# Gate tiles of the V stage loaded in three pieces, the first ones ahead of the last block's gathers

## The chip, the cores and the metric

The kernel runs on one core of a Trainium2 chip. The metric is the time of one execution in microseconds (us), taken on the device; the median of several runs stands for a kernel. The engines are named as in the profile: PE multiplies matrices, PEld loads its weights, DVE and ACT work on tiles element by element, POOL and SP mostly issue transfers here. Transfers (DMA) run on 16 DMA engines that all the issuing queues share.

## What is computed

The reference is one decoder layer on 512 tokens of width 1024: a mixer (state-space heads and latent attention), and then an expert mixer called PEER, which is the part that matters here. Each token picks 128 experts out of 16384 (8 heads, 16 each). With `u_table` and `v_table` of 16384 rows of 1024 numbers:

```python
        u = jnp.take(u_table, expert_idx, axis=0)
        act = jax.nn.gelu(jnp.einsum('td,thkd->thk', xb, u).astype(jnp.float32), approximate=False)
        v = jnp.take(v_table, expert_idx, axis=0)
        return jnp.einsum('thk,thkd->td', (gate * act).astype(xb.dtype), v)
```

## The kernel before

The mixer takes the first quarter of the span. PEER then works in two ways at once. For the first 384 tokens it doesn't gather: it computes the activation of every expert for every token with dense matmuls, multiplies by a gate that is zero for experts that were not picked, and multiplies the result with the whole V table. For the last block of 128 tokens it gathers the picked rows of U and V with indirect transfers on POOL (`gather`, L1534 to L1584) and sums on DVE. In fp32 each matrix is split into a high and a low part, so each product takes three matmuls.

The 16384 experts are cut into 128 chunks of 128. A U step (`u_chunk`) takes one 512 KB piece of U and makes the activations of a chunk for the tokens, 128 experts by 352 numbers, with 24 matmuls. A V step (`v_chunk`, L1678) takes one 512 KB piece of V and adds into six PSUM banks with 18 matmuls. The weights come through one stream (`Stream`, L94): SP issues the load of a raw piece `wir` (L105, three buffers), ACT rounds it to the high part `wih` (L123), DVE subtracts for the low part `wil` (L133). SP issues the next load into a raw buffer when DVE has read it.

Before the V steps the gates are built and stored to memory: `gsp`, 12 groups of 32 tokens by 128 by 128 chunks by 32, and the small `gs0` for the first eight chunks of the last two groups. For a V step they are loaded as a tile `gt`, which holds four chunks for all 12 groups of 32 tokens (128 by 12 by 4 by 32, 768 KB), in two buffers. `load_g(q)` loads the tile of the chunks 4q to 4q+3. For the first two tiles POOL loads the part of the last two groups out of `gs0`. For later tiles SP loads from `gsp`. As long as some groups were multiplied already while the gates were built (`open_(c)` counts the groups that are open at chunk c, up to `ND` = 10), only the open groups and the last two are loaded; from chunk 40 on (tile 10) all 12 are, in one transfer of 768 KB.

`v_prep(c)` (L1622) asks for the tile of c and, at every fourth chunk, for the next one, and multiplies activations by gates into `P` on DVE (L1632; for c from 40 on all in one instruction), with a small copy on ACT (L1636). `v_hi` rounds P to `Ph` on ACT (L1655), `v_lo` makes `Pl` on DVE (L1663), and `v_mm` (L1667) multiplies them with the V piece. In a V step c the order written out is: `v_lo` of the chunk before, `v_prep(c + 2)`, the next weight piece with `item()`, `v_hi(c + 2)`, and 18 matmuls.

The stages in time: until about 810 us mixer, routing, gates and the first U steps; four V steps alone; then U and V steps in turn until the U pieces are used up, near 1300 us; then V steps alone. Beside all of them `pump` advances the gathers of the last block, paced by the steps that are left.

Around the start of the V steps the order is: the generator `gather` runs to its first stop (DVE makes `ac`), then to its second (POOL issues the gathers of rows 0 and 1), then `load_g(0)` and `load_g(1)`, then the gather of row 2, then `refill`, which fetches activations that had been put away in memory (L1402).

Of the kernel before, what the change touches and what calls it, by code (L numbers as in the profile page):

```python
# [49 lines left out]
T_Q = 6.3  # L50
ROWS = 5
ENDU = 11
WV = 0.86
GST = (1, 3, 5, 7)
LOWA = (*range(2, 32, 2), 34, 38)
# [12 lines left out]
def tile_block(ctx: ExitStack, tc: tile.TileContext, I, out):  # L68
    nc = tc.nc
# [20 lines left out]
    def chain(*gs):  # L90
        for g in gs:
            yield from g
# [139 lines left out]
    gsp = dram.tile([NT // 32, 128, 128, 32], F32, name="gsp")  # L232
# [74 lines left out]
    for p in range(2):  # L307
# [11 lines left out]
        for j, cs, act in (((0, slice(0, D), 1), (1, slice(0, D), 1)) if p == 0 else  # L319
                           ((0, slice(0, D), 0), (1, slice(0, 512), 1), (1, slice(512, D), 0))):  # L320
            t = XH[:, 2 * p + j, cs]
# [355 lines left out]
    for i in range(13, 18):  # L677
# [3 lines left out]
        q = qraw[i - 13] = wk.tile([128, S], F32, name="qr", bufs=5)  # L681
# [210 lines left out]
    for st in range(39):  # L892
        h, q = divmod(st, 4)
# [141 lines left out]
    def stage1(m):  # L1035
        yield top16(sc.pop(m), 128, TV4[:, :, m], TI4[:, :, m])
        h = m // 2
        if m % 2:
            cand = rt.tile([128, NB, 88], F32, name="cand")
            for c0, a0, na, w in ((0, 0, 1, 16), (16, 1, 3, 8), (40, 4, 12, 4)):  # L1040
                sh = [128, NB, na, w]
                (V if m == 15 else G).tensor_tensor(
                    cand[:, :, c0:c0 + na * w].rearrange("p h (a b) -> p h a b", a=na),
                    TV4[:, :, m - 1, a0:a0 + na, None].to_broadcast(sh),
                    TV4[:, :, m, None, 0:w].to_broadcast(sh), op=OP.add)
            late_c.append((cand, h))
        if late_c and (m % 2 == 0 or m == 15):
            cand, h = late_c.pop()
            yield (0.7 if m == 15 else 0.0) + top16(cand, 88, TS4[:, :, h], PO4[:, :, h])
# [276 lines left out]
    def pump(g, us):  # L1326
        bal[0] = min(bal[0] + us, us)
        while bal[0] > 0:
            c = next(g, None)
            if c is None:  # L1330
                bal[0] = 0.0
                return False
            bal[0] -= c
        return True
# [61 lines left out]
    def refill():  # L1396
        while away:
            t = act_tile()
            if t is None:
                return  # L1400
            c = away.pop(0)
            G.dma_start(t, asp[c - KEEP])  # L1402
            ACT[c] = t
# [82 lines left out]
    fill = iter(())  # L1486
    for m in range(17):
# [6 lines left out]
        if m:  # L1494
            fill = chain(fill, stage1(m - 1))
# [91 lines left out]
    aps.append(pool("act3"))  # L1587
    fill = gather()
    next(fill)
    next(fill)  # L1590
    gt = {}

    open_ = lambda c: sum(d <= c for d in done)
# [1 line left out]
    def load_g(q):  # L1595
        if q < 32 and q not in gt:
            gt[q] = vst.tile([128, NT // 32, 4, 32], F32, name="gt", bufs=2)
            nb = open_(q * 4)
            part = lambda b0, b1: nc.sync.dma_start(gt[q][:, b0:b1], gsp[b0:b1, :, q * 4:q * 4 + 4, :].rearrange("b j i t -> j b i t"))
            if q < 2:  # L1600
                G.dma_start(gt[q][:, ND:].rearrange("j b i t -> j b (i t)"), gs0[:, q])
            elif nb < ND:
                part(ND, NT // 32)
            if nb:
                part(0, nb if q < 2 or nb < ND else NT // 32)

    for q in range(2):
        load_g(q)
    next(fill)
    refill()  # L1610
    if UO:
# [10 lines left out]
    def v_prep(c):  # L1622
        load_g(c // 4)
        if c % 4 == 0:
            load_g(c // 4 + 1)
        a = ACT.pop(c)
        P = vst.tile([128, NT], F32, name="P", bufs=2)
        nb = open_(c)
        for b0, b1 in ((0, ND + 1),) if nb == ND else ((0, nb), (ND, ND + 1)):
            if b1 > b0:  # L1630
                cs = slice(b0 * 32, b1 * 32)
                V.tensor_tensor(P[:, cs].rearrange("p (b t) -> p b t", t=32), a[:, cs].rearrange("p (b t) -> p b t", t=32),  # L1632
                                gt[c // 4][:, b0:b1, c % 4, :], op=OP.mult)
        if nb < ND:
            A.activation(P[:, nb * 32:ND * 32], a[:, nb * 32:ND * 32], AF.Copy)
        A.activation(P[:, NA:], gt[c // 4][:, ND + 1, c % 4, :], AF.Copy)  # L1636
        if c % 4 == 3:
            gt.pop(c // 4)
        prepared[0] += 1
        return P  # L1640
# [37 lines left out]
    def v_chunk(c):  # L1678
        v_lo()
        P = v_prep(c + 2)  # L1680
        if uc == 128:
            v_hi(c + 2, P)
        hl = item()
        if uc < 128:
            v_hi(c + 2, P)
        for b in range(3):
            v_mm(b, c, hl)
# [3 lines left out]
    for c in range(2):  # L1691
        while uc < PRE - 1 + c:
            u_chunk(uc)
            uc += 1
            if uc > un[0] + 2:
                pump(fill, 2.3)
        v_hi(c, v_prep(c))
        v_lo()
    more = True
    units = lambda: (128 - uc) * 2 + WV * (uc - vc)  # L1700
    fin = None
    while vc <= LASTC:
# [14 lines left out]
        else:  # L1717
            if not GS[1]:
                GS[1:] = units() - ENDU, GS[0]
            left = units()  # L1720
            want = 253 - max(0.0, (256 - GS[2]) * (left - ENDU) / GS[1])
            while more and GS[0] < want:
                more = pump(fill, 0.1)
            if more and left < ENDU:
                more = pump(fill, 1.8)
# [9 lines left out]
    for c in range(LASTC + 1, 128):  # L1735
        v_lo()
        if c + 2 < 128:
            v_hi(c + 2, v_prep(c + 2))
        held[c] = item()
# [135 lines left out]
```

## Time and profile before

| | us |
|---|---|
| median of 3 runs | 1581.57 |
| lowest and highest | 1578.41, 1581.69 |
| profiled execution | 1585.28 |
| its span, first to last instruction | 1583.5 |

The profile is of one execution, so durations are compared with its own span. In the page, the first part gives each engine's busy time, share and instructions. A row of the timeline has start, duration, engine, line, operation, what is written and read, the count, and in brackets the idle time of the engine before it with what ended it. In the waits, a row names who waited for whom, the total, the times and the longest. For a transfer the duration in the timeline is that of its issue; when it has landed is seen by who was released.

### The profile page before, as it was taken

What the parts mean: (1) busy time and instruction counts of PE and PEld (TensorE: products, weight loads), DVE (VectorE), ACT (ScalarE), POOL (GpSimd) and SP (SyncE); (2) the same over time, 40 slices, a digit from 0 to 9 for tenths busy, and PEclk for the clock granted to TensorE, in tenths of its full rate; (3) what the DMA queues carried; (4) which work ended last, traced back from release to release, by engine and by line L of the source; (5) the groups of instructions that cost most, each with busy time, mean ns of one, the idle gap of its engine ahead of it and who ended that gap; (6) DMA issues with size and microseconds to landing.
All of it is one profiled execution on the core that took longest, in us unless ns stands there. A gap on an engine that the chain in (4) does not pass through costs nothing.

```text
span 1583.5 us, 24521 instructions
## 1 busy us (share of the span) xinstructions
PE 1550.6 (98%) x8696; PEld 1361.3 (86%) x8696; DVE 1344.2 (85%) x2620; ACT 767.6 (48%) x1536; POOL 619.2 (39%) x455
## 2 busy tenths in 40 slices
PE   9999999999999999999989999999999999999997
PEld 7887888888888999999988999999988878888886
DVE  8988767747799999999957888888888889998997
ACT  5565476741433547776754444444333344443442
POOL 0000032500245434443225655565555556655510
PEclk9999999999999999999999999999999999999999
DMA  6242122474423568999989999999999999999983
GB/s 252 94 160 90 47 76 63 124 238 145 125 86 101 153 211 299 329 328 340 330 314 313 359 344 351 358 364 351 338 339 352 351 350 348 375 363 349 354 284 145
DMA packets 150442, 407.53 MB, mean 257 GB/s; under 512 B 14360, under 2 KB 55528, under 8 KB 150064
## 3 DMA queue, kind: packets, MB, share of 16 engines
q1 hardware_dynamic: 94160, 208.91, 39.2%
q0 software_dynamic: 50288, 177.80, 31.2%
q10 hardware_dynamic: 5872, 19.27, 3.2%
q8 instruction: 68, 1.11, 0.3%
q14 instruction: 54, 0.44, 0.1%
HBM read 374.63 MB, written 29.19 MB: 255 GB/s over the span
## 4 chain that ended last, share of the span: by engine, by line
PE 79%; DVE 7%; DMA 6%; issue 5%; ACT 2%; POOL 2%; DVEq 0%; ACTq 0%; POOLq 0%
PE pu L86 9%; PE va L1672 9%; PE va L1673 9%; PE va L1676 9%; PE pu L88 9%; PE pu L87 9%; PE pa L87 3%; PE pa L88 3%; PE pa L86 3%; PE pw L87 3%; PE pw L88 3%; PE pw L86 3%; DMA row<-v,ix 2%; POOL row L1550 2%; PE pw L1283 1%
## 5 line engine op out<-in xcount | busy, mean ns | idle before, releaser
L123 ACT ACTIVATE wih<-wir 128x1024 fp32r<-128x1024 f32 (+2 forms) x269 | 277.8, 1033 | 226.7 <-DMA wir<-v 94.6
L133 DVE TENSOR_TENSOR wil<-wir,wih 128x1024 fp32r<-128x1024 f32 (+1 forms) x234 | 283.0, 1212 | 76.7 <-ACT wih L123 55.4
L88 PE MATMUL pu<-XT,wil 128*128 128x336 f32 x1008 | 319.0, 316 | 4.5 <-DVE wil L133 4.5
L1673 PE MATMUL va<-wil,Ph 128*128 128x512 f32 x726 | 284.2, 391 | 0.0
L86 PE MATMUL pu<-XT,wih 128*128 128x336 f32 x864 | 276.5, 320 | 3.0 <-ACT wih L123 3.0
L87 PE MATMUL pu<-XT,wih 128*128 128x336 f32 x864 | 272.8, 316 | 0.0
L1550 POOL DMA_INDIRECT row<-v,ix x128 | 207.2, 1619 | 155.4 <-DVE ac L1571 132.3
L1550 POOL DMA_INDIRECT row<-u,ix x128 | 190.0, 1484 | 159.5 <-DVE row L1565 105.1
L88 PEld LDWEIGHTS pu<-XT,wil 128*128 128x128 f32 x1008 | 189.8, 188 | 5.7 <-DVE wil L133 5.6
L1672 PE MATMUL va<-wih,Ph 128*128 128x512 f32 x462 | 181.6, 393 | 4.3 <-ACT Ph L1655 4.3
L1571 DVE SCALAR_TENSOR_TENSOR ac<-row,hd,ac 128x1024 f32<-128x1024 f32 x128 | 164.1, 1282 | 7.9 <-DMA row<-v,ix 6.1
L86 PEld LDWEIGHTS pu<-XT,wih 128*128 128x128 f32 x864 | 162.7, 188 | 6.5 <-ACT wih L123 4.3
L87 PEld LDWEIGHTS pu<-XT,wih 128*128 128x128 f32 x864 | 163.0, 189 | 2.1
L1673 PEld LDWEIGHTS va<-wil,Ph 128*128 128x128 f32 x726 | 137.2, 189 | 27.3 <-DVE wil L133 0.3
L1565 DVE SCALAR_TENSOR_TENSOR row<-row,XT 128x1024 f32<-128x1024 f32 x128 | 150.4, 1221 | 8.1 <-DMA row<-u,ix 8.0
L1676 PE MATMUL va<-wih,Pl 128*128 128x512 f32 x462 | 143.7, 392 | 2.2 <-DVE Pl L1663 2.2
L133 POOL TENSOR_TENSOR wil<-wir,wih 128x1024 fp32r<-128x1024 f32 (+3 forms) x35 | 72.9, 2089 | 154.7 <-PE pw L88 99.4
L123 ACT ACTIVATE wihx<-wir 128x1024 fp32r<-128x1024 f32 x67 | 71.1, 1062 | 121.1 <-DMA wir<-v 96.5
L1146 POOL DMA_INDIRECT urow<-u,uix x48 | 77.2, 1609 | 115.3 <-DVE urow L1152 108.1
L1655 ACT ACTIVATE Ph<-P 128x384 fp32r<-128x384 f32 x121 | 62.9, 520 | 108.3 <-DVE P L1632 74.3
L133 DVE TENSOR_TENSOR wil<-wir,wihx 128x1024 fp32r<-128x1024 f32 x62 | 75.8, 1223 | 40.5 <-issue 19.2
L1672 PEld LDWEIGHTS va<-wih,Ph 128*128 128x128 f32 x462 | 87.3, 189 | 21.9 <-ACT Ph L1655 4.5
(513 smaller groups left out, 3419.0 us busy)
## 6 DMA issues: line engine op xcount, KB each, us to landing
wir<-ut SPq DMA_DIRECT2D x128, 512.0 KB
wir<-v SPq DMA_DIRECT2D x128, 512.0 KB
gt<-gsp SPq DMA_DIRECT2D x22, 768.0 KB
wir<-wo SPq DMA_DIRECT2D x26, 512.0 KB
wir<-wf SPq DMA_DIRECT2D x18, 512.0 KB
wir<-wqr SPq DMA_DIRECT2D x16, 512.0 KB
gsp<-stg ACTq DMA_DIRECT2D x14, 464.0 KB
de<-acd POOLq DMA_DIRECT2D x8, 512.0 KB
```

What stands on the lines that cost most here:

```text
L86: T.matmul(ps, lh, rh, start=start, stop=False)
L87: T.matmul(ps, lh, rl, start=False, stop=False)
L88: T.matmul(ps, ll, rh, start=False, stop=stop)
L123: A.activation(h, r, AF.Copy)
L133: self.lo(n).tensor_tensor(l, r, h, op=OP.subtract)
L1146: G.indirect_dma_start(out=UR[n], out_offset=None, in_=I["u"], in_offset=bass.IndirectOffsetOnAxis(ap=UR["ix"][:, n:n + 1], axis=0))
L1550: G.indirect_dma_start(out=R[s], out_offset=None, in_=I["u"] if s < 128 else I["v"], in_offset=bass.IndirectOffsetOnAxis(ap=ix3[:, s % 128 ...
L1565: V.scalar_tensor_tensor(wide(r), wide(r), 1.0, x3, op0=OP.mult, op1=OP.mult, accum_out=hd[:, s:s + 1])
L1571: V.scalar_tensor_tensor(ac, r, hd[:, s - 128:s - 127], ac, op0=OP.mult, op1=OP.add)
L1672: T.matmul(va[b][e], Ph[b], h[:, cs], start=c == 0, stop=False)
L1673: T.matmul(va[b][e], Ph[b], l[:, cs], start=False, stop=False)
L1676: T.matmul(va[b][e], Pl[b], h[:, cs], start=False, stop=c == 127)
```

## The change

A number `GP` = 4 is the size of a piece in token groups. Loads on SP are not issued in `load_g` any more but put into a list `more_g`. `step_g` takes one entry off it, issues up to four groups, and puts the rest back at the front; if an entry was small and the next one fits with it into four groups, it issues that one too. `v_prep` calls `step_g` once each time, after `load_g`. A whole tile so goes out as three loads of four groups (256 KB each), with the V steps 4q, 4q+1 and 4q+2 for the tile that is first used by the multiply of chunk 4q+4. At the start of the stage, `load_g(0)`, `load_g(1)` and all that they put on the list now come after the first stop of `gather` and ahead of the second.

```diff
+GP = 4
     fill = gather()
     next(fill)
-    next(fill)
     gt = {}
...
-            part = lambda b0, b1: nc.sync.dma_start(gt[q][:, b0:b1], gsp[b0:b1, :, q * 4:q * 4 + 4, :].rearrange("b j i t -> j b i t"))
+            part = lambda b0, b1: more_g.append((q, b0, b1))
             if q < 2:
                 G.dma_start(gt[q][:, ND:].rearrange("j b i t -> j b (i t)"), gs0[:, q])
...
+    more_g = []
+
+    def step_g():
+        if more_g:
+            q, b0, b1 = more_g.pop(0)
+            m = min(b1, b0 + GP)
+            nc.sync.dma_start(gt[q][:, b0:m], gsp[b0:m, :, q * 4:q * 4 + 4, :].rearrange("b j i t -> j b i t"))
+            if m < b1:
+                more_g.insert(0, (q, m, b1))
+            elif more_g and m - b0 + more_g[0][2] - more_g[0][1] <= GP:
+                step_g()
+
     for q in range(2):
         load_g(q)
+    while more_g:
+        step_g()
+    next(fill)
     next(fill)
     refill()
...
         load_g(c // 4)
         if c % 4 == 0:
             load_g(c // 4 + 1)
+        step_g()
```

## The prediction

> **What bounds the kernel now.** I read the page first, for the engine that has least room.
>
> ```profile
> span 1583.5 us, 24521 instructions
> ...
> PE 1550.6 (98%) x8696; PEld 1361.3 (86%) x8696; DVE 1344.2 (85%) x2620; ACT 767.6 (48%) x1536; POOL 619.2 (39%) x455
> ...
> gt<-gsp SPq DMA_DIRECT2D x22, 768.0 KB
> ```
>
> PE is busy for 98% of the span. A change that touches no matmul can win only the time in which PE stands still or runs at a lower clock. So the second view is that of the waits of PE, asked for in stretches; its columns are the total in us, the times and the longest.
>
> ```profile
> PE va L1672 <- ACT Ph L1655: 4.3, 1, 4.3
> ```
>
> ```profile
> PE pu L88 <- DVE wil L133: 4.5, 4, 2.8
> PE pu L86 <- ACT wih L123: 3.0, 3, 1.2
> PE va L1676 <- DVE Pl L1663: 2.2, 2, 2.0
> ```
>
> The first is the answer for 800 to 830 us, the second that for 1160 to 1310 us. Between 900 and 1160 us, and from 1310 to 1530 us, the view has no row. So PE loses 4.3 us at the first V step and 9.7 us (4.5 + 3.0 + 2.2) in one stretch of 150 us. The third view is the busy time by window: span of the window, then PE, PEld, DVE, ACT, POOL, the granted clock, the DMA share and GB/s.
>
> ```profile
> 820.00:840.00 20.00, 15.74 (x68) 13.00 (x67) 8.22 (x15) 9.39 (x22) 9.46 (x12) 0.91 1.01 377
> 1060.00:1080.00 20.00, 20.00 (x108) 17.98 (x107) 17.42 (x30) 8.71 (x19) 11.45 (x8) 1.00 0.98 365
> 1160.00:1180.00 20.00, 16.55 (x78) 14.46 (x78) 14.09 (x15) 8.10 (x15) 8.18 (x7) 0.91 0.83 298
> 1300.00:1320.00 20.00, 17.98 (x72) 14.17 (x71) 18.73 (x22) 7.13 (x13) 13.80 (x7) 0.91 0.97 348
> 1310.00:1530.00 220.00, 220.00 (x972) 182.17 (x971) 202.95 (x239) 89.94 (x164) 123.70 (x71) 1.00 1.00 356
> ```
>
> The clock falls with the long waits: 0.91 over 20 us is (1 - 0.91) x 20 = 1.8 us of clock in each of three windows, one of the first place and two of the second. What there is to win is therefore 4.3 + 1.8 = 6.1 us at the first step and 9.7 + 2 x 1.8 = 13.3 us in the stretch, 19.4 us together.
>
> The Trainium skill (TensorE: Matmul & The Clock Gate, Part 1, and the table under "Why this matters for your kernels") lets the clock fall after an idle time of about 3.4 us and asks for no gap over some 3 us; by that only the first wait would cost clock, and the sum would be 3.6 us smaller. The trace disagrees: the windows with waits of 2.8 and 2.0 us also show 0.91.
>
> **The first loads of the gates.** The chain of work that ended last, from 812 us on (start, us, what), says why PE waits there.
>
> ```profile
> 812.11 2.08 DMA gs<-stg
> ...
> 815.45 10.45 DMA gt<-gs
> 825.91 0.23 ACT P L1636
> 826.20 0.53 ACT Ph L1655
> 826.78 0.51 PE va L1672
> ```
>
> The timeline of POOL, and that of PE, give the order.
>
> ```profile
> 812.21 1.97 POOL L1550 DMA_INDIRECT row<-u,ix  x1 [28.80 <-DVE ac L1543]
> 814.48 0.96 POOL L1550 DMA_INDIRECT row<-u,ix  x1 [0.30 <-DMA gs<-stg]
> 815.45 1.18 POOL L1601 DMA_DIRECT2D gt<-gs  x2
> 816.93 1.17 POOL L1550 DMA_INDIRECT row<-u,ix  x1 [0.30 <-issue]
> 824.27 2.72 POOL L1402 DMA_DIRECT2D act<-asp  x5 [6.17 <-DMA asp<-aout]
> ```
>
> ```profile
> 822.20 0.32 PE L88 MATMUL pu<-XT,wil 128*128 128x336 f32 x1
> 826.78 0.51 PE L1672 MATMUL va<-wih,Ph 128*128 128x512 f32 x1 [4.26 <-ACT Ph L1655]
> ```
>
> Two gathered rows of 512 KB stand ahead of the two small gate loads (256 KB together) in POOL's queue. The change puts the gate loads first. They can't be issued before the store gs<-stg has landed, at 812.11 + 2.08 = 814.19, so they go out about 1.2 us sooner; what counts is that 1 MB is no longer ahead of them. The packets by queue show when POOL's queue (q0) was served at all: between 812 and 819 us it has no row, and from 819 to 822 us it has this one.
>
> ```profile
> q0 software_dynamic: 142, 0.53, 43.4%
> ```
>
> At 0.53 MB in 3 us, 0.26 MB of gates at the head of the queue take 1.5 us: they are through at about 820.5 us, and land at 820.5 to 822 (up to 1.5 us for the tail is an estimate; gs<-stg took 2.08 us from issue to landing in all). From the landing to the matmul it takes 826.78 - 825.90 = 0.9 us, and PE is free at 822.4, so a landing by 821.5 leaves no wait and one at 822 leaves 0.5 us. The bounds are 6.1 us (no wait) and nothing (the load lands at 825.9 as now, held by the stores that fill the other queues). I take 5.5 us.
>
> What is moved with it: the gathers 0 and 1 go out behind the wait for gs<-stg and behind 1.18 us of gate issues, some 3.5 us later than 812.21. Their cover is the idle 6.17 us of POOL ahead of 824.27 and the first use of a row, which DVE makes here:
>
> ```profile
> 841.66 1.22 DVE L1565 SCALAR_TENSOR_TENSOR row<-row,XT 128x1024 f32<-128x1024 f32 x1
> ```
>
> Even if that comes 6 us sooner, the rows have 18 us. Without this cover each us of delay would be a us of DVE. No gate load on SP is moved at this place: the line L1599 starts with tile 2, at 834 us. What is late next is the following weight piece, whose split on DVE stood behind the same wait and so moves with it. Cost taken: nothing.
>
> **The gate tiles in three pieces.** Each whole tile is a load of 768 KB, on the queue that brings the weights. SP's timeline and ACT's show what it does, and a stretch before has the natural comparison: while few blocks were open, a tile came as two small loads.
>
> ```profile
> 1050.30 0.95 SPq L1599 DMA_DIRECT2D gt<-gsp  x2
> 1052.82 0.34 SPq L105 DMA_DIRECT2D wir<-ut  x1
> ...
> 1216.23 0.43 SPq L1599 DMA_DIRECT2D gt<-gsp  x1
> 1218.56 3.91 SPq L105 DMA_DIRECT2D wir<-ut  x1
> ```
>
> ```profile
> 1061.14 1.06 ACT L123 ACTIVATE wih<-wir 128x1024 fp32r<-128x1024 f32 x1 [1.00 <-DMA wir<-ut]
> ...
> 1233.12 1.06 ACT L123 ACTIVATE wih<-wir 128x1024 fp32r<-128x1024 f32 x1 [7.32 <-DMA wir<-ut]
> ```
>
> ```profile
> gt<-gsp SPq DMA_DIRECT2D x1, 192.0 KB
> gt<-gsp SPq DMA_DIRECT2D x1, 128.0 KB
> ```
>
> Behind 320 KB of gates (192 + 128, the issues of 1050 to 1052 us) a weight piece took 1061.14 - 1052.82 = 8.3 us from its issue to ACT, and PE never waited. Behind 768 KB it took 1233.12 - 1218.56 = 14.6 us, of which SP spent 3.91 instead of 0.34 us in the issue itself, and PE waited behind ACT and DVE. A piece of 256 KB is smaller than that harmless case, but it comes in three V steps of four, and the engines have little spare: a share of 0.98 at 1060 us without a wait, 1.00 in the V-only stretch, again without one. The average load does not change, only its lumps. So the two bounds of this part are 13.3 us (every wait goes) and nothing (the queue is as full as before, and the lateness is only spread). By the nearest row, the 8.3 us, nearly all goes; for the fuller queue I keep 2.3 us of waits and take 11.0 us.
>
> What it adds: two more issues for each of 22 tiles, 44 at the 0.43 us of a whole one, 19 us of SP over 450 us. SP mostly waits for DVE anyway:
>
> ```profile
> SPq L105 <- DVE wil L133: 532.5, 169, 10.8
> ```
>
> (800 to 1560 us), so this costs nothing; without that cover a weight piece would be 0.4 us later. Tiles 2 to 9, with their small loads, change only in order, and no wait of PE stands there. The multiply P on DVE now waits for three landings instead of one, and behind it in DVE's order stand the weight splits and the gathers' sums, for which PE and POOL wait. The last piece is the risk, below.
>
> **Sum.** 5.5 + 11.0 = 16.5 us. The profiled execution took 1585.28 us (a span of 1583.5 and 1.8 around it) and would come to 1568.8; it stands 3.7 us above the median of the runs, 1581.57, from which the forecast is counted: 1565 us.
>
> **Rivals.** *The queue stays full.* In the u and V stretch the DMA share is already near 1, PE asks for the same bytes in fewer us once it no longer waits, and weight pieces come late in small steps instead of one large one. Against it stands that at 1160 to 1180 us the share fell to 0.83 just when PE waited: there was room, at another time. Half or less of the 13.3 us would come, 1 to 6.5 us, with the 5.5 us of the first place 6.5 to 12 us in all: 1569.5 to 1575, chance 0.13. At its end stands a case of its own: with the engines full the splitting gives nothing at all, since every byte still has to pass, and only the 5.5 us come, 1576, chance 0.05. The Trainium skill (Perfetto Trace Analysis, DMA Optimizations) names splitting as a help where the DMA engines are generally idle, which they are not here, at 0.97 to 1.01 in four of the five windows; that rule speaks for this last case, and the share of 0.83 against it.
>
> *The first gate load stays late*, because the stores ahead in the other queues and not the gathers hold it. For it speaks that q0 got nothing before 819 us. Then only 11 us come: 1570.5. Chance 0.07.
>
> *The last piece is late: slower.* In the V-only stretch the third piece goes out two V steps before its use. SP's, DVE's and ACT's rows bound it.
>
> ```profile
> 1327.11 3.56 SPq L105 DMA_DIRECT2D wir<-v  x2
> ...
> 1357.36 0.33 SPq L105 DMA_DIRECT2D wir<-v  x1
> ```
>
> ```profile
> 1339.68 0.52 DVE L1632 TENSOR_TENSOR P<-acts,gt 128x352 f32<-128x352 f32 x1
> ```
>
> ```profile
> 1367.90 1.06 ACT L123 ACTIVATE wihx<-wir 128x1024 fp32r<-128x1024 f32 x1 [4.58 <-DMA wir<-v]
> ```
>
> It would be issued with the second of the two pieces at 1327.11, at about 1330.3, for the multiply at 1339.68: a lead of 9.4 us. The slowest weight piece near by took 1367.90 - 1357.36 = 10.5 us, but behind a whole tile. DVE is busy 203 of 220 us there, so a period of four steps (16.3 us) has 1.2 us to spare. Beyond a landing of 9.4 + 1.2 = 10.6 us each further us is lost on each of 14 tiles. To eat the 16.5 us it must be 11.8 us on the average, to be slower by 3.2 us, 12.0. At 12.5 us the loss is 14 x 1.9 = 26.6, net 10 us slower: 1591.7. A piece of a third of the size makes that unlikely. Chance 0.05.
>
> *It doesn't move the bound*: the waits come back elsewhere and the sum is within 0.2%. Chance 0.05.
>
> **How the numbers follow.** The forecast (13 to 20 us won: 1561.5 to 1568.5) has 0.65. The range takes in the full 19.4 us below with a little for the scatter of the runs, 1560.5, and above the first rival and the second, up to 1575; outside are the slower case, no change, the splitting that gives nothing, and edges of the others, some 0.2 together. 0.2%, 3.2 us, is about what a measurement of this kernel can tell from no change. Faster: 0.65 + 0.13 + 0.05 + 0.07 = 0.90; same 0.05; slower 0.05.
>
> **What would show it.** The wait of PE for Ph near 822 us gone or under 1 us, and 1.00 for the clock there; gt<-gs issued ahead of the first row on POOL. In 1160 to 1310 us the three rows of waits under 3 us together, the weight piece behind a gate piece issued in 0.34 us and landing after some 8 us instead of 14.6. DVE must show no wait of P for gt<-gsp in the V-only stretch. It is wrong if PE's waits in that stretch keep more than half of their 9.7 us, or if new waits of P appear.

## The result, and the profile after

| | before | after |
|---|---|---|
| median, us | 1581.57 (5 runs, 1578.41 to 1582.97) | 1564.49 (5 runs, 1563.93 to 1564.82) |
| profiled execution, us | 1585.28 | 1564.62 |
| its span, us | 1583.5 | 1562.9 |

The ratio of the times is 0.9897, with a 95% interval of 0.9882 to 0.9911: 17.1 us less at the medians. The profiled executions differ by 20.7 us, because the one of before, 1585.28 us, was longer than every one of its five runs. The runs of the changed kernel also lie closer together, 0.9 us from lowest to highest against 4.6 us.

The page of the kernel after, its first part:

```profile
span 1562.9 us, 24588 instructions
...
PE 1544.5 (99%) x8696; PEld 1358.9 (87%) x8696; DVE 1344.5 (86%) x2620; ACT 767.6 (49%) x1536; POOL 595.6 (38%) x455
```

PE does the same 8696 matmuls in 1544.5 instead of 1550.6 us of busy time and with less idle time around them. The mean granted clock of the two executions, 0.999 after and 0.995 before, accounts for that difference in busy time: 0.004 x 1550 = 6.2 us. Where the idle time was, the view of PE's waits, from 800 to 1560 us, now has two rows (total, times, longest):

```profile
PE va L1688 <- ACT Ph L1671: 0.6, 1, 0.6
PE va L1689 <- DVE wil L134: 0.3, 1, 0.3
```

The first is the wait at the first V step, 4.3 us before. The three rows of the u and V stretch, 9.7 us together, are gone. (The code has moved down: L1688 was L1672, L1671 was L1655, L134 was L133.) The windows, with span, PE, PEld, DVE, ACT, POOL, clock, DMA share and GB/s:

```profile
820.00:840.00 20.00, 19.37 (x93) 16.27 (x92) 10.07 (x17) 10.96 (x24) 7.78 (x13) 1.00 1.03 400
...
1160.00:1310.00 150.00, 150.00 (x775) 133.16 (x775) 140.28 (x146) 61.68 (x117) 87.51 (x60) 1.00 1.01 375
...
1310.00:1530.00 220.00, 220.00 (x972) 182.08 (x971) 202.21 (x254) 91.85 (x174) 97.69 (x69) 1.00 0.96 338
```

The clock is 1.00 where it was 0.91, and PE is busy for all of the 150 us in which it had stood still for 9.7. The same window of before had this row:

```profile
1160.00:1310.00 150.00, 140.31 (x710) 122.72 (x710) 126.79 (x129) 56.52 (x109) 78.40 (x56) 0.98 0.95 344
```

So 775 instead of 710 matmuls pass in the same 150 us, and the DMA engines move 375 instead of 344 GB/s to feed them: there was room in the engines, only not at the right time. (The two windows don't hold quite the same steps: the last U matmul starts at 1271 us after the change and at 1288 before.)

The chain of work that ended last shows the first V step (start, us, what):

```profile
814.69 7.21 DMA gt<-gs
...
821.92 0.23 ACT P L1652
...
822.20 0.53 ACT Ph L1671
...
822.78 0.50 PE va L1688
```

The gate load now lands 7.21 us after its issue instead of 10.45, at 821.9. POOL's timeline has it ahead of the first gathered row:

```profile
814.69 1.10 POOL L1601 DMA_DIRECT2D gt<-gs  x2 [31.66 <-DMA gs<-stg]
816.09 1.63 POOL L1551 DMA_INDIRECT row<-u,ix  x1 [0.30 <-issue]
```

And SP's timeline shows a weight piece behind a gate piece, issued in 0.33 us where it took up to 3.91:

```profile
1177.08 0.43 SPq L1613 DMA_DIRECT2D gt<-gsp  x1
1179.52 0.33 SPq L106 DMA_DIRECT2D wir<-ut  x1
```

ACT's timeline has its arrival, which no longer holds anybody up for long:

```profile
1187.87 1.06 ACT L124 ACTIVATE wih<-wir 128x1024 fp32r<-128x1024 f32 x1 [1.19 <-DMA wir<-ut]
```

That is 1187.87 - 1179.52 = 8.4 us from issue to ACT, against 14.6 in the case quoted of before.

### The profile page after: what moved, and what is told of

The parts are those of the page before. It is cut to its first block, busy times and chain, and to the rows that moved or that the text cites. A ratio compares the mean times of both kernels' runs of the same rounds, so it can differ in the third digit from the quotient of the medians.

```text
span 1562.9 us, 24588 instructions
## 1 busy us (share of the span) xinstructions
PE 1544.5 (99%) x8696; PEld 1358.9 (87%) x8696; DVE 1344.5 (86%) x2620; ACT 767.6 (49%) x1536; POOL 595.6 (38%) x455
## 4 chain that ended last, share of the span: by engine, by line
PE 89%; DVE 6%; ACT 2%; DMA 1%; issue 1%; DVEq 0%; ACTq 0%; POOLq 0%
PE pu L87 11%; PE pu L89 10%; PE pu L88 10%; PE va L1688 10%; PE va L1689 10%; PE va L1692 10%; PE pa L89 3%; PE pa L88 3%; PE pa L87 3%; PE pw L88 3%; PE pw L89 3%; PE pw L87 3%; PE pw L1284 1%; PE pw L1285 1%; PE pb L536 1%
## 5 line engine op out<-in xcount | busy, mean ns | idle before, releaser
L134 DVE TENSOR_TENSOR wil<-wir,wih 128x1024 fp32r<-128x1024 f32 (+1 forms) x234 | 282.7, 1210 | 74.4 <-ACT wih L124 45.0
L1551 POOL DMA_INDIRECT row<-v,ix x128 | 191.8, 1498 | 159.3 <-DVE ac L1572 131.2
L1551 POOL DMA_INDIRECT row<-u,ix x128 | 185.8, 1452 | 125.6 <-DVE row L1566 99.0
L1688 PE MATMUL va<-wih,Ph 128*128 128x512 f32 x462 | 180.2, 390 | 0.6 <-ACT Ph L1671 0.6
L134 POOL TENSOR_TENSOR wil<-wir,wih 128x1024 fp32r<-128x1024 f32 (+3 forms) x35 | 72.9, 2089 | 154.3 <-PE pw L89 99.3
L1671 ACT ACTIVATE Ph<-P 128x384 fp32r<-128x384 f32 x121 | 62.6, 518 | 130.7 <-DVE P L1648 65.3
L1147 POOL DMA_INDIRECT urow<-u,uix x48 | 73.2, 1524 | 119.5 <-DVE urow L1153 112.5
L134 DVE TENSOR_TENSOR wil<-wir,wihx 128x1024 fp32r<-128x1024 f32 x62 | 75.7, 1222 | 35.1 <-issue 21.6
L1688 PE MATMUL va<-wihx,Ph 128*128 128x512 f32 x264 | 103.0, 390 | 0.0
```

Of the source, the lines that this page charges most:

```text
L134: self.lo(n).tensor_tensor(l, r, h, op=OP.subtract)
L1147: G.indirect_dma_start(out=UR[n], out_offset=None, in_=I["u"], in_offset=bass.IndirectOffsetOnAxis(ap=UR["ix"][:, n:n + 1], axis=0))
L1551: G.indirect_dma_start(out=R[s], out_offset=None, in_=I["u"] if s < 128 else I["v"], in_offset=bass.IndirectOffsetOnAxis(ap=ix3[:, s % 128 ...
L1688: T.matmul(va[b][e], Ph[b], h[:, cs], start=c == 0, stop=False)
```

## The experiments

**One part at a time.** First the pieces without the new order: the second stop of `gather` comes ahead of the gate loads again.

```diff
     fill = gather()
     next(fill)
+    next(fill)
     gt = {}
...
     while more_g:
         step_g()
     next(fill)
-    next(fill)
     refill()
```

> The pieces stay, the first gate loads go back behind the gathers of rows 0 and 1. If the two parts of the change are independent and sized as predicted (5.5 us and 11 us of 16.5), this loses the 5.5 us again: 1570 us, with PE's wait for Ph of some 4 us back near 822 us, a clock of 0.91 in that window, and no wait of PE from 1160 to 1310 us. Rival: PE's early start is given back later, since the DMA engines set the pace of the U and V stretch; then the place of the first load is worth nothing and this runs in 1564 to 1566 us, as the whole change does.

Measured: 1570.93 us (ratio to before 0.9934, 0.9919 to 0.995), 6.4 us above the whole change. (The kernel before, run beside this kernel and the second, third and fourth below, had a median of 1581.64 us, as in the first result, so their medians can be set against 1564.49.) PE's waits from 800 us on:

```profile
PE va L1688 <- ACT Ph L1671: 4.5, 1, 4.5
PE va L1689 <- DVE wil L134: 0.3, 1, 0.3
```

The wait at the first V step is back; the 0.3 us are in the changed kernel too. The window of that wait shows what the clock adds:

```profile
820.00:840.00 20.00, 15.53 (x62) 12.67 (x61) 8.22 (x15) 9.37 (x22) 7.54 (x12) 0.83 0.97 357
```

At 0.83 the clock took (1 - 0.83) x 20 = 3.4 us here, more than the 1.8 of the first profile of before. With the wait of 4.5 us in place of 0.6 these rows make 7.3 us, 0.9 more than the medians show. The rival, that the early start is given back later, falls.

Then the new order without the pieces:

```diff
-GP = 4
+GP = 12
...
-        step_g()
+        while more_g:
+            step_g()
         a = ACT.pop(c)
```

> The new order at the start, but whole tiles of 768 KB (GP = 12, all of a tile in its first step). If the lump on SP's queue is what makes PE wait later, the three rows of waits between 1160 and 1310 us come back, 7 to 13 us with the clock, and the time is 1574 to 1577 us. Rival: the waits of that stretch were an echo of the late start (the gathers and weights pushed 4 to 6 us behind); then they are gone here too and the time is 1565 us.

Measured: 1574.44 us (0.996, 0.9945 to 0.9975), 9.9 us above the whole change. The waits of the stretch are back, fewer than in the first profile of before (4.9 us in all, against 9.7):

```profile
PE va L1693 <- DVE Pl L1680: 2.5, 1, 2.5
PE pu L87 <- ACT wih L124: 1.2, 1, 1.2
PE pu L89 <- DVE wil L134: 1.2, 2, 0.7
```

With a clock of 0.99 over the 150 us, 1.5 us more, that is 6.4 us, a little under the 7 us expected; the profile is of the shortest of six runs, 1571.93 us. So the waits are no echo of the late start: they are there without it, and the kernel with the late start had none. The two parts add up: 6.4 + 9.9 = 16.3 us, of 17.1.

**Smaller, or spread out?** The third kernel keeps the transfers of 256 KB but sends all three in one V step:

```diff
-        step_g()
+        while more_g:
+            step_g()
         a = ACT.pop(c)
```

> As the changed kernel, but the three pieces of 256 KB go out one right after the other in the first V step of four, not one per step. Theory (the bytes ahead of a weight piece on SP's queue): as with whole tiles, weight pieces behind them take 13 to 14 us, PE waits 7 to 13 us with the clock, 1574 to 1577 us. Rival (the transfer of 1536 packets in one instruction holds up SP's issue of the next weight piece by 2.6 to 3.9 us, and smaller transfers don't): the pieces alone help, 1564 to 1567 us.

Measured: 1575.24 us (0.9959, 0.9943 to 0.9976), as with whole tiles. PE's waits in the stretch are back, 6.3 us of them, one of 2.3 us at its start:

```profile
PE va L1693 <- DVE Pl L1680: 3.4, 2, 2.0
PE pu L89 <- DVE wil L134: 2.9, 2, 2.3
```

SP's timeline shows that the issue of the next weight piece is held about as long as behind a whole tile:

```profile
1142.06 1.59 SPq L1613 DMA_DIRECT2D gt<-gsp  x3
1143.76 3.43 SPq L106 DMA_DIRECT2D wir<-ut  x1
```

The kernel with whole tiles has these rows there:

```profile
1140.78 0.43 SPq L1613 DMA_DIRECT2D gt<-gsp  x1
1142.45 2.71 SPq L106 DMA_DIRECT2D wir<-ut  x1
```

It is 3.43 us and 2.71, against the usual 0.33; over the five tiles from 1140 to 1280 us it is 1.9 to 3.4 us here and 2.5 to 3.7 with whole tiles. ACT starts on these two weight pieces at 1156.69 and 1153.76, 12.9 and 11.3 us after their issue. So the hold comes with the 768 KB that go out together, in one instruction or in three; whether the bytes count or the packets they are cut into, no run separates. Splitting alone buys nothing; that the pieces go out in different steps does.

**Whose queue?** The fifth kernel leaves the tile whole and at its old place, but ACT issues it (and `GP` = 12 and the loop as above):

```diff
-            nc.sync.dma_start(gt[q][:, b0:m], gsp[b0:m, :, q * 4:q * 4 + 4, :].rearrange("b j i t -> j b i t"))
+            nc.scalar.dma_start(gt[q][:, b0:m], gsp[b0:m, :, q * 4:q * 4 + 4, :].rearrange("b j i t -> j b i t"))
```

> Whole tiles of 768 KB at their old places, but issued by ACT, on its own queue, with the new order at the start. If what hurts is that the weight pieces stand behind the tile in SP's own queue, they pass it here: SP issues each in 0.34 us, few or no waits of PE between 1160 and 1310 us, 1564 to 1568 us. Rival: all queues share the 16 DMA engines, and a lump of 768 KB delays the weights from any queue; then PE waits 7 to 13 us with the clock as with whole tiles on SP, 1573 to 1577 us.

Measured: 1568.58 us (0.9929, 0.99 to 0.9958), between the two theories, with runs from 1564.2 up to 1582.6. SP issues its weight pieces in 0.33 us again up to 1260 us, and PE's waits are smaller but not gone (the 0.7 us is that of the first V step):

```profile
PE va L1693 <- DVE Pl L1680: 1.5, 2, 0.8
PE va L1690 <- DVE wil L134: 0.8, 1, 0.8
PE va L1689 <- ACT Ph L1672: 0.7, 1, 0.7
PE pu L89 <- DVE wil L134: 0.5, 1, 0.5
PE va L1689 <- ACT wih L124: 0.4, 1, 0.4
```

Weight pieces still come late, though no tile stands ahead of them in SP's queue. The one issued at 1237.24 us, 2.2 us behind a tile on ACT, reaches ACT after 10.7 us:

```profile
1247.97 1.06 ACT L124 ACTIVATE wih<-wir 128x1024 fp32r<-128x1024 f32 x1 [9.06 <-DMA wir<-v]
```

So standing in SP's own queue is a part of the harm, and not all of it. The medians (1574.44 to 1568.58, of the 9.9 us) would make it the larger part. But the two intervals overlap, this kernel ran on another chip than the one with whole tiles, and ACT issues the tile in its own order and so at another moment of the step: how large each part is isn't shown.

**How close is the slower rival?** The fourth kernel sends each piece one V step later, by calling `step_g` ahead of `load_g`:

```diff
+        step_g()
         load_g(c // 4)
         if c % 4 == 0:
             load_g(c // 4 + 1)
-        step_g()
```

> Each piece goes out one V step later (steps 4q+1 to 4q+3), so the last one has a single V step until its multiply. This tests the rival that ended slower. In the V-only stretch the lead falls from about 9.4 to 5.3 us, pieces land after 7 to 9 us, so P on DVE waits 2 to 3.5 us in each of 14 tiles; with 1.2 us to spare per tile that is 1 to 2.3 us each, 14 to 32 us in all: 1578 to 1596 us, with a row DVE P waiting for DMA gt<-gsp. Rival: the two steps that P and the weights are ahead of the matmuls cover it, DVE waits but PE doesn't: 1564 to 1567 us.

Measured: 1584.1 us (1.0028, 1.0009 to 1.0048): slower than the kernel before. Its profiled execution, at 1579.63 us one of the faster, shows the new wait of DVE from 1300 us on, and the second fence PE's waits from 800 us on:

```profile
DVE P L1648 <- DMA gt<-gsp: 22.4, 9, 4.0
```

```profile
PE va L1692 <- DVE Pl L1679: 4.0, 2, 2.0
PE va L1688 <- ACT act L1671: 2.2, 1, 2.2
PE va L1688 <- ACT Ph L1671: 1.3, 2, 0.7
```

Not every tile is hit, as I had reckoned, but each hit can be larger (up to 4.0 us). The same change, one step of some 4 us later, loses all that it wins. PE's waits explain part of that: 8.0 us in all instead of 0.9, where the profiled executions differ by 15.0. In the changed kernel the same view of DVE, from 1130 to 1560 us, has one wait of this kind:

```profile
DVE P L1648 <- DMA gt<-gsp: 0.5, 1, 0.5
```

**How many pieces?** With `GP` = 6, two pieces of 384 KB in two steps:

> GP = 6: two pieces of 384 KB in the first two V steps of four. If the delay of a weight piece grows with the bytes ahead of it (8.3 us behind 320 KB, 14.6 us behind 768 KB in the trace of before, PE waiting only behind the second), 384 KB is near the harmless case: PE waits 0 to 4 us, 1564.5 to 1569 us. Rival: what counts is that the load is spread evenly over the steps, so two steps of four are half as good as three: 1568 to 1572 us.

Measured: 1564.29 us, four runs from 1564.03 to 1567.89 (0.9902, 0.9867 to 0.9936). The rival, two steps half as good as three (1568 to 1572 us), falls. The profile is of the longest of the four and has one wait of PE of 2.2 us for a low part, near 1160 us. To tell whether that is chance, two and three pieces ran in the same rounds once more.

> GP = 6 once more, in more rounds. If 384 KB is at the edge (one wait of 2.2 us in its first profile, none in three of four times), most runs are within 1 us of the changed kernel and some 2 to 4 us above, median 1564 to 1566. Rival: two pieces are as good as three, then no run is above 1565.5.

> The changed kernel once more, on the same chip and in the same rounds as two pieces. If no wait of PE is left that depends on how transfers happen to meet, it comes back at 1564 to 1565 us with a scatter of 1 us, while the kernel before scatters by 5 us or more beside it.

Measured: two pieces 1566.62 us (1564.19 to 1568.76; 0.9917, 0.9899 to 0.9934), the changed kernel 1565.26 us (1563.92 to 1565.8; 0.9908, 0.9892 to 0.9924), beside a kernel before at 1580.05 us. The intervals overlap, so it isn't shown that three pieces beat two. Two pieces reach the same lowest time, but four of the six runs are 2 to 5 us longer. Both expectations missed: most runs were to be within 1 us of the changed kernel and the median at 1566 at most, and by the rival no run above 1565.5. The profile again has one wait at the same place:

```profile
PE pu L89 <- DVE wil L134: 1.8, 1, 1.8
```

The scatter of the changed kernel was 1.9 us here, more than the 1 us that I had named, with no wait in its profile beyond the two of 0.6 and 0.3 us.

**Why the kernel before scatters.** It was profiled once more:

> The kernel before, profiled once more. The runs of before scatter by 5 us and more, those of the changed kernel by 1 us. If the scatter is that of PE's waits behind the large loads, this profile shows another sum of waits between 1160 and 1310 us than the 9.7 us of the first, and its time differs from 1585.3 by about that difference and its clock; the 4.3 us at 822 us stay. Rival: the scatter lies elsewhere (start, end, clock), and the sum of waits is 9.7 us again whatever the time.

Measured: 1580.32 us. PE's waits from 800 us on:

```profile
PE va L1672 <- ACT Ph L1655: 4.4, 1, 4.4
PE pu L88 <- DVE wil L133: 3.8, 3, 2.8
PE va L1676 <- DVE Pl L1663: 2.0, 1, 2.0
PE pu L86 <- ACT wih L123: 0.2, 1, 0.2
```

and the windows of the two places:

```profile
820.00:840.00 20.00, 15.62 (x62) 12.80 (x61) 8.22 (x15) 9.37 (x22) 8.47 (x12) 0.83 1.00 367
1160.00:1310.00 150.00, 143.84 (x737) 126.49 (x736) 130.18 (x135) 57.52 (x111) 82.69 (x58) 0.99 0.97 353
```

The first wait is as long as ever; the others come to 6.0 instead of 9.7 us. That is 3.7 us of the 5.0 by which this execution is shorter than the first one. The clock explains 0.01 x 150 = 1.5 us more in the stretch, but at the first step it cost 0.08 x 20 = 1.6 us more than in the first profile, so 1.4 us stay unexplained. Two profiles can't prove it, but they fit a reading in which the first wait is fixed by the order of the program (4.3, 4.4 and, with the old order put back, 4.5 us) and the others depend on how transfers happen to meet.

## Why the prediction was right

It said 1565 us, and 1564.49 was measured; the likeliest case came, with both parts, near the size of each. That the sum was met within 1 us is in part luck. The 16.5 us were read from an execution of 1585.28 us and taken off a median 3.7 us lower, though the second profile says that such an execution is longer mostly by the waits that the change removes: the 3.7 us were in good part taken off twice. Counted within the one execution, the working said 1568.8, and 1564.62 came. Against this error stood others of the opposite sign, named below.

- *The first gate load.* Said: it goes out when gs<-stg has landed, lands at 820.5 to 822, leaves 0 to 0.5 us of wait, and is worth 5.5 us. Measured: landed at 821.9, 0.6 us of wait, clock at 1.00, and 6.4 us by the experiment that takes it away. The clock was the part that was set too low: I reckoned 1.8 us from one profile, and two other executions had 0.83 in that window, 3.4 us.
- *What was moved.* The gathers went out later (816.09 instead of 812.21 us), and this cost nothing: from 800 to 860 us DVE has no wait for a gathered row. POOL waits twice for one to land, 1.0 us in all.
- *The pieces.* Said: of 13.3 us of waits and clock 11 go and 2.3 stay. Measured: none stays, yet the part is worth 9.9 us. Here a size was off, in a term and its remainder, which cancel in part: the 13.3 us were those of an execution 3.7 us above the median, and the second profile shows another with 6.0 instead of 9.7 us of waits. With the clock over the 150 us (0.98 and 0.99) the two executions had 12.7 and 7.5 us to win there, and 9.9 lies between.
- *The nearest row.* The 8.3 us behind 320 KB stood for the weight piece behind 256 KB; 8.4 us was read off above. That three such loads in four steps would be one too many, the case of the full queue, didn't come: the DMA share in the stretch rose from 0.95 to 1.01 without a wait. The Trainium skill's condition for splitting (Perfetto Trace Analysis, DMA Optimizations: engines generally idle) isn't met here, with a share of 0.95, and the change helped. That doesn't go against the page: with three pieces at once smaller transfers alone did nothing; what helped was to send them in different steps.
- *The slower rival.* I gave the last piece a lead of 9.4 us and a landing in time; the page of the kernel after gives 8.3 us as the median from issue to landing.

```profile
gt<-gsp SPq DMA_DIRECT2D x66, 256.0 KB, 8.3
```

That is about 1 us of margin, and one wait of 0.5 us, at 1301 us. The prediction had asked for no such wait after the last U step and named new waits of P as a sign of being wrong; by the letter this one is such a wait, but PE has no wait from 1160 to 1530 us, so it cost nothing. The chance of 0.05 was for the placement as it is; one step further the rival holds, as the fourth kernel shows. Its price was reckoned as 14 to 32 us for the later placement and came out at 1584.1 - 1564.5 = 19.6.

## What to carry to other kernels

Where an engine is busy 98% of the time, list its waits and the clock around them: without touching its work that is all there is to win. A cause that comes back every four steps shows itself by its period: before, SP's issue was held behind the gate tiles at 1150.6, 1185.2, 1218.6 and 1253.2 us. A large load in the queue that also brings urgent pieces should be spread over the steps, not only cut up: three pieces sent together were as bad as one. Reckon the lead of the last piece against the measured landing before moving it, since one step can turn the gain into a loss; and where runs scatter by nearly as much as a term that is added up (4.6 us here, for a term of 5.5), take the terms from more than one profile.

## What was not expected

- The clock after a wait of about 2 us is not the same each time. In the first profile of before a wait of 2.0 us was followed by 0.91 over 20 us. In the two profiles of two pieces, a wait of 2.2 us near 1160 us left it at 1.00, and a shorter one of 1.8 us at the same place brought 0.91:

```profile
1150.00:1170.00 20.00, 17.78 (x97) 15.89 (x96) 16.12 (x21) 7.18 (x14) 9.14 (x7) 1.00 0.93 334
1150.00:1170.00 20.00, 18.17 (x89) 16.30 (x88) 14.41 (x19) 7.74 (x15) 7.99 (x6) 0.91 0.91 323
```

The Trainium skill (TensorE: Matmul & The Clock Gate, Part 1) counts activity in a free-running window of some 3.4 us; a window whose phase differs from run to run would fit the difference, which no run here tests. It doesn't explain why a wait shorter than that window lowers the clock at all, and these rows show that it can.
- With room in the engines, the share of the DMA engines can be 1.01 over 150 us at 375 GB/s without one wait of PE, while at 0.95 it waited nine times (4 + 3 + 2): the share alone didn't tell whether transfers were the limit.
